# Moving the context feed-forward's buffers, and its operand preparation, in a two-layer hybrid transformer kernel on one Trainium2 core

## The chip, the cores and the metric

The kernel runs on one core of one Trainium2 chip. The metric is device time in microseconds for one execution, the median of several. The core has five engines with a queue of instructions each: TensorE (PE in the profile: matmuls, with its weight loads listed as PEld), VectorE (DVE), ScalarE (ACT), GpSimd (POOL) and SyncE (SP, which here only issues transfers). An engine runs its own instructions strictly in order; semaphores make it wait for others. Transfers between HBM and SBUF are carried by 16 DMA engines.

## What is computed

Two layers over a latent sequence of 1024 tokens (`x`) and a context of 256 tokens (`ctx`), width 1024, all in float32. Each layer: modulated RMS norm, a mixer (layer 0 recurrent, layer 1 attention), a gated residual, and a convolutional feed-forward with a gated residual. The modulation vectors come from the conditioning vectors by one matrix of 1024 x 6144 a layer. What bears on this case is the end of layer 0:

```python
def _ada(cond, w, b):
    m = (jax.nn.silu(cond) @ w + b)[:, None, :]
    return jnp.split(m, 6, axis=-1)

def _conv_ffn(h, w_up, conv_w, w_down):          # D_FF = 2816
    gate, val = jnp.split(h @ w_up, 2, axis=-1)
    gate = _dwconv(gate, conv_w)
    return (jax.nn.silu(gate) * val) @ w_down

for i in range(DEPTH):                           # DEPTH = 2
    ...
    x = x + ml[2] * mix_l
    x = x + ml[5] * _conv_ffn(_modulate(_rms(x), ml[3], ml[4]), ffn_w_up[i], ffn_conv[i], ffn_w_down[i])
    if not last:
        ctx = ctx + mc[2] * mix_c
        ctx = ctx + mc[5] * _conv_ffn(_modulate(_rms(ctx), mc[3], mc[4]), ffn_w_up[i], ffn_conv[i], ffn_w_down[i])
return _rms(x) * final_norm
```

## The kernel before

The kernel is one straight program in stages. Those around the change are, in program order:

- **Mixer output** (lines 1263 to 1325): the output projection of layer 0's mixer, first for the context chunk (`ci` 0, plain float32), then for the two latent chunks (`ci` 1 and 2, each float32 operand split in a high and a low part, three matmuls a product by `mm3`, lines 155 to 157). `m_in(0)` loads the context's mixer result into the tile `m0`, `m_in(1)` and `m_in(2)` go through the load buffers `mt`. In this stage the operand `hx` of the next one is made.
- **Context feed-forward** (lines 1328 to 1349, with `ffn_ctx`, lines 1207 to 1253): 22 steps `step(f)`, one for each 128 hidden columns. A step loads the gate's and the value's 1024 x 128 weights in two buffers of 256 KB each, multiplies them with `hx` (line 1220, tile `fg`) and applies convolution, SiLU and product on ACT and DVE (tile `ft`). Every fourth step, and the last, multiplies the finished groups by their down weights (`downs`, line 1230, tile `fd`) and adds the result to `xT[0]`. A float32 matmul shows as two records.
- Two generators are advanced between the steps. `mods` (`mod_chain`, `mod_steps`) makes the modulation vectors of layer 1: 24 pieces of 8 rows each, 192 advances; an advance loads 128 KB from GpSimd's queue (line 217, tile `mw`) and multiplies and adds it on DVE into `macc`, for both conditioning vectors in the first 8 pieces and for one in the others; a piece ends with matmuls (line 230, tile `mps`) that run when the next piece is at its second advance. `prep` (`ffn_prep`) makes the operands of the next stage from `xT[1]` and `xT[2]`: 20 advances, each some work on ACT, DVE, GpSimd and a few matmuls, through the scratch tiles `rm_sq`, `rm_rs`, `rm_dg`.
- Inside a step `fill()` advances `mods` by two, twice a step and twice more in each `downs`; after a step, `prep` is advanced by one and `mods` by four.
- **First feed-forward** (lines 1350 to 1377, `ffn_run`): layer 0's feed-forward on the 1024 latent tokens, again 22 steps `up(f)`, by seven products of split operands each. `up(f)` loads the two weight tiles (`st`, 512 KB each), splits them into `w0h`/`w0l` (gate) and `w1h`/`w1l` (value) by a cast on ACT (line 1100) and a subtraction on GpSimd, then adds and subtracts the two weight tiles in place on DVE (`st<-st`, line 94) and splits each result (`s0` to `s3`, line 1109). The products with `w0` come first, then `s0`, `s1`, ... After `up(0)` the hook `ctx_out` normalises the finished context and writes it out.

Order and memory are not written out by hand. A scheduler lays out each engine's queue by simulating the program: an instruction goes in as soon as its operands and its buffer are free, the earlier in program order first. Pools of SBUF tiles are stacks: a pool opened with `side="right"` is put below the right stack, any other on top of the left stack, in the order of the calls, and a pool's buffers are used in turn. A tile on an address that a closed pool had waits for the earlier tiles there, tile by tile (`reuse_waits="tile"`), and for nothing else.

In bytes of a partition, from the shapes: the left stack holds 14,048 bytes (constants and `xT0`), then `h0` with `m0` and `hx` (8,192 each). On it the mixer output stage puts `tmpc` (10,304), `fstc` and `fstw` (8,192 each: the two buffers of the input and of the weight loads), then `mi` (four `mt`), `wo`, `mpc`. The context stage puts `fsta` (11 weight buffers of 2,048), `mpa` (four `macc`, six `mw`, 10,240), `fga` (six `ft`, 6,144), `fta` (2,048) and `tmpa` (`prep`'s scratch, 10,304), up to 81,696. The right stack comes down to 81,888 with `xT1`, `xT2` and the operands of the first feed-forward. Below that come, when the context stage is over, the first feed-forward's own pools: `fst0` (load buffers, 10,240), `fw0` (split weights, 28,672, in the order `w0h`, `w0l`, `w1h`, `w1l`, `s0h` to `s3l` from below), `ft0` (12,320).

Of the kernel before, what the change touches and what calls it, by code (L numbers as in the profile page):

```python
# [9 lines left out]
F32 = mybir.dt.float32  # L10
# [9 lines left out]
KD = 8  # L20
# [50 lines left out]
def kernel(  # L71
# [9 lines left out]
    def dma(o, i):  # L81
        o = o.bitcast(F32) if o.dtype == F32R else o
        i = i.bitcast(F32) if i.dtype == F32R else i
        nc.sync.dma_start(out=o, in_=i)

    def dump(name, ap):
        if dbg is not None and name in dbg:
            dma(dbg[name], ap)
# [4 lines left out]
    def tt(e, o, a, b, op):  # L93
        e.tensor_tensor(out=o, in0=a, in1=b, op=op)  # L94
# [7 lines left out]
    def stt(e, o, a, s, b, op0, op1):  # L102
        e.scalar_tensor_tensor(out=o, in0=a, scalar=s, in1=b, op0=op0, op1=op1)  # L103

    def pool(stack, name, bufs, psum=False, side=None):
        kw = {"space": PSUM} if psum else {}
        return stack.enter_context(tc.tile_pool(name=name, bufs=bufs, reuse_waits="tile", side=side, **kw))
# [37 lines left out]
    def evac(i, o, a):  # L145
        if i % 2 == 0:
            S.copy(out=o, in_=a)
        else:
            V.tensor_copy(out=o, in_=a)

    def hilo(pl, shape, name):
        return [pl.tile(shape, F32R, tag=f"{name}{e}", name=f"{name}{e}") for e in "hl"]

    def mm3(ps, wh, wl, xh, xl, first, last):
        T.matmul(ps, lhsT=wh, rhs=xh, start=first, stop=False)  # L155
        T.matmul(ps, lhsT=wh, rhs=xl, start=False, stop=False)  # L156
        T.matmul(ps, lhsT=wl, rhs=xh, start=False, stop=last)  # L157

    def split(hi, lo, src, lo_eng=None):
        S.copy(out=hi, in_=src)  # L160
        tt(lo_eng or G, lo, src, hi.bitcast(F32), ALU.subtract)
# [39 lines left out]
    def rms_mod(tmp, psp, tag, xt, n, s1, sh, hi, lo, w=256):  # L201
        for p0 in range(0, n, w):
            xs = xt[:, :, p0:p0 + w]
            r, sq = normalised(tmp, psp, tag, xs)
            tt(V, sq, xs, r, ALU.mult)
            if lo is None:
                scale_shift(hi[:, :, p0:p0 + w], sq, s1, sh)
            else:
                modulate(sq, s1, sh, hi[:, :, p0:p0 + w], lo[:, :, p0:p0 + w])
# [45 lines left out]
    def mod_acc(*a):  # L255
        for _ in mod_steps(*a):
            pass

    def mcol(l, d, idx):
        return modc[l][d][:, idx * 8:idx * 8 + 8]  # L260
# [14 lines left out]
    with ExitStack() as p0:  # L275
        ini = p0.enter_context(tc.tile_pool(name="ini", bufs=1, reuse_waits="tile"))
        ld = p0.enter_context(tc.tile_pool(name="ld", bufs=2, reuse_waits="tile"))
        tmp = p0.enter_context(tc.tile_pool(name="tmp0", bufs=1, reuse_waits="tile"))
# [743 lines left out]
    def ffn_ops(pl):  # L1022
        Ah = hilo(pl, [128, KD, 2, 256], "a")
        Bh = hilo(pl, [128, 4, 2, 256], "b")
        return Ah, Bh, [hilo(pl, [128, 4, 2, 256], f"t{i}") for i in range(4)]
# [50 lines left out]
    def load(p, src):  # L1076
        st = p.st.tile([128, KD, 128], F32, tag="st", name="st")
        dma(st, src)
        return st
# [178 lines left out]
    if True:  # L1258
        fa, fc = Ffn(), Ffn()
        xp0 = pool(p0, "xp0", 1)  # L1260
        xT[0] = xp0.tile([128, KD, NCTX], F32, name="xT0")
        h0 = pool(h0s, "h0", 1)
        with ExitStack() as po:
            hC = pool(po, "hC", 1, side="right")
            tmp = pool(po, "tmpc", 1)
            fc.st = pool(po, "fstc", 2)
            fw = Ffn()
            fw.st = pool(po, "fstw", 2)
            mi = pool(po, "mi", 4)
            wo = pool(po, "wo", 5)  # L1270
            mp = pool(po, "mpc", 1)
            mhl = {}
            def x_in(g):
                src = ctx_in[0, g:g + 128] if g < NCTX else x[0, g - NCTX:g - NCTX + 128]
                ci, o = (0, g) if g < NCTX else ((g - NCTX) // 512 + 1, (g - NCTX) % 512)
                xin = load(fc, src.rearrange("p (k m) -> p k m", m=128))
                for hf in range(2):
                    ps = pd.tile([128, 4, 128], F32, tag="d", name="xtr")
                    for k in range(4):
                        T.transpose(ps[:, k], xin[:, hf * 4 + k], ident)  # L1280
                    evac(hf, xT[ci][:, hf * 4:hf * 4 + 4, o:o + 128], ps)

            xs_ = iter(range(0, NT, 128))
            def m_in(ci):
                t0, n = CHUNKS[ci]
                if ci == 0:
                    mf = mhl[0] = h0.tile([128, KD, n], F32, tag="m0h", name="m0")
                    for k in KORD:
                        dma(mf[:, k], m_scr[k, :, t0:t0 + n])
                    return  # L1290
                mh, ml_ = mhl[ci] = hilo(hC, [128, KD, n], f"m{ci}")
                for k in KORD:
                    mt = mi.tile([128, 512], F32, tag="mt", name="mt")
                    dma(mt[:, 0:n], m_scr[k, :, t0:t0 + n])
                    S.copy(out=mh[:, k], in_=mt[:, 0:n])
                    tt(V, ml_[:, k], mt[:, 0:n], mh[:, k].bitcast(F32), ALU.subtract)
            for ci in (0, 1, 2):
                m_in(ci)
            for _ in range(6):
                x_in(next(xs_))  # L1300
            for ci in (0, 1, 2):
                t0, n = CHUNKS[ci]
                d = 1 if ci == 0 else 0
                if ci not in (0, 1, 2):
                    m_in(ci)
                for dt in range(KD):
                    st = load(fw, rec_w_out[0, :, dt * 128:(dt + 1) * 128].rearrange("(k p) m -> p k m", p=128))
                    ps = pu.tile([128, 512], F32, tag="u", name="po")
                    if ci == 0:
                        for i, k in enumerate(KORD):  # L1310
                            T.matmul(ps[:, 0:n], lhsT=st[:, k], rhs=mhl[0][:, k], start=i == 0, stop=i == KD - 1)
                    else:
                        mh, ml_ = mhl[ci]
                        wh, wl = hilo(wo, [128, KD, 128], "wo")
                        split(wh, wl, st)
                        for i, k in enumerate(KORD):
                            mm3(ps[:, 0:n], wh[:, k], wl[:, k], mh[:, k], ml_[:, k], i == 0, i == KD - 1)
                    stt(V, xT[ci][:, dt], ps[:, 0:n], mcol(0, d, 2)[:, dt:dt + 1], xT[ci][:, dt], ALU.mult, ALU.add)
                    for _ in range({(0, d): 1 for d in range(2, 6)}.get((ci, dt), 0)):
                        x_in(next(xs_))  # L1320
                dump(f"xmix{ci}", xT[ci])
                mod_acc(mp, pd, "d", 0, (4, 3, 5)[ci], (0, 1), 0, 1024)
                if ci == 1:
                    hx = h0.tile([128, KD, NCTX], F32, tag="m0l", name="hx")
                    rms_mod(tmp, pd, "d", xT[0], NCTX, mcol(0, 1, 4), mcol(0, 1, 3), hx, None, w=128)
        if stop == "C":
            return
        hEs = ExitStack()
        ops = ffn_ops(pool(hEs, "hE0", 1, side="right"))
        with ExitStack() as pf:  # L1330
            fa.st = pool(pf, "fsta", 11)
            mp = pool(pf, "mpa", 1)
            mods = mod_chain([(mp, pd, "d", 1, i, (0, 1) if i < 2 else (0,), q, 256, 6, nc.gpsimd) for i in (1, 0, 2, 4, 3, 5) for q in range(4)])
            fa.g = pool(pf, "fga", 6)
            fa.t = pool(pf, "fta", 2)
            step = ffn_ctx(fa, hx, lambda: (next(mods, None), next(mods, None)))
            tmp = pool(pf, "tmpa", 1)
            prep = (None for ci in (1, 2) for _ in ffn_prep(0, ops, tmp, ci, 128))
            for f in range(NF):
                step(f)  # L1340
                next(prep, None)
                for _ in range(4):
                    next(mods, None)
            for _ in prep:
                pass
            for _ in mods:
                pass
            dump("xf0_0", xT[0])
        h0s.close()
    pf = ExitStack()  # L1350
# [30 lines left out]
    with ExitStack() as pq:  # L1381
# [5 lines left out]
        with ExitStack() as pqq:  # L1387
# [35 lines left out]
            with ExitStack() as pt_q:  # L1423
                tmp = pool(pt_q, "tmpq", 2, side="right")
# [179 lines left out]
    with ExitStack() as pe:  # L1604
# [3 lines left out]
        with ExitStack() as pr_:  # L1608
            tmp = pool(pr_, "tmpe", 1)
# [65 lines left out]
```

## Time and profile before

| | us |
|---|---|
| median of 3 runs | 3424.66 (3417.45 to 3427.35) |
| the profiled execution | 3425.41 |
| span of the profiled execution's instructions | 3423.6 |
| PE busy, share of the span | 93% |
| DVE, POOL, ACT busy | 70%, 45%, 38% |

A view of the profile is either a total (busy time of an engine, of a group of instructions, of a stretch of the span) or an order of events (the timeline, where each row is a run of equal instructions on one engine, with the idle time before it in brackets and what ended it). PE's busy time is modelled and says little about how full PE is; the count of matmuls in a stretch says more. Times in the timeline are microseconds from the span's start; the context feed-forward runs from 1122 to 1383.

### The profile page before, as it was taken

How to read it: one execution, taken by the hardware profiler on the slowest of the kernel's cores; microseconds unless marked ns; L12 is line 12 of the kernel's file. 1: busy time of each engine (PE TensorE's matmuls, PEld its weight loads, DVE VectorE, ACT ScalarE, POOL GpSimd, SP SyncE). 2: the span in 40 equal slices, each digit the busy share in tenths (PEclk: the TensorE clock that was granted, in tenths of full speed). 3: DMA queues.
4: the chain of work that ended last, by engine and by line, in shares of the span. 5: the costliest groups of instructions: out<-in, count | busy, mean ns of one | idle time of the engine just before them, and what ended most of it. 6: DMA issues, size and time to landing. Idle time of an engine off the chain costs nothing. (4 is left out here: it accounts for less than half of the span.)

```text
span 3423.6 us, 47533 instructions
## 1 busy us (share of the span) xinstructions
PE 3188.8 (93%) x16708; PEld 2667.4 (78%) x16708; DVE 2394.2 (70%) x4177; ACT 1309.6 (38%) x2982; POOL 1535.8 (45%) x1459
## 2 busy tenths in 40 slices
PE   7988988899979999899999997999999799999998
PEld 4776877777768888688887877988888678887877
DVE  5567467568767877777767777467567667777677
ACT  4434242644421222333333323557566433333333
POOL 2232231233215455565555643753434555655554
PEclk9998999999979999999999998999999899999999
DMA  5445444645586677211121121330111111111211
GB/s 185 112 123 162 135 128 126 185 146 166 178 267 198 192 242 229 72 56 44 53 59 50 56 71 45 105 90 26 50 44 35 28 53 50 56 44 53 59 50 71
DMA packets 438508, 350.14 MB, mean 102 GB/s; under 512 B 57556, under 2 KB 385470, under 8 KB 437758
## 3 DMA queue, kind: packets, MB, share of 16 engines
q1 hardware_dynamic: 429054, 321.93, 31.6%
q0 software_dynamic: 9216, 25.18, 2.3%
q8 instruction: 132, 2.16, 0.3%
q14 instruction: 106, 0.87, 0.1%
HBM read 286.25 MB, written 60.76 MB: 101 GB/s over the span
## 5 line engine op out<-in xcount | busy, mean ns | idle before, releaser
L103 DVE SCALAR_TENSOR_TENSOR xT<-fd,mod,xT 128x512 f32<-128x512 f32 (+1 forms) x432 | 291.4, 694 | 192.7 <-PE fd L157 170.5
L155 PE MATMUL pj<-hhi,whi 128*128 128x512 f32 (+1 forms) x696 | 263.8, 379 | 22.2 <-ACT raw L525 13.1
L156 PE MATMUL fd<-gl,dh 128*128 128x512 f32 (+1 forms) x688 | 266.7, 388 | 6.1 <-DVE gl L94 6.0
L157 PE MATMUL fd<-gh,dl 128*128 128x512 f32 (+1 forms) x688 | 266.1, 387 | 0.0
L155 PE MATMUL fd<-gh,dh 128*128 128x512 f32 (+1 forms) x688 | 262.0, 391 | 0.6 <-ACT gh L1155 0.3
L156 PE MATMUL pj<-hlo,whi 128*128 128x512 f32 (+1 forms) x696 | 260.9, 375 | 0.3 <-DVE hlo L94 0.3
L157 PE MATMUL pj<-hhi,wlo 128*128 128x512 f32 (+1 forms) x696 | 259.4, 373 | 0.0
L94 DVE TENSOR_TENSOR st<-st 128x512 f32<-128x512 f32 x176 | 211.7, 1204 | 51.2 <-POOL s1l L94 39.2
L103 DVE SCALAR_TENSOR_TENSOR macc<-mw,sc,macc 128x256 f32<-128x256 f32 (+1 forms) x322 | 206.9, 668 | 32.5 <-DMA mw<-in_mod_w_dram 30.9
L100 POOL TENSOR_SCALAR P<-P,rc 128x512 f32<-128x512 f32 (+1 forms) x192 | 116.7, 626 | 200.0 <-DVE rc L1539 57.6
L94 POOL TENSOR_TENSOR dl<-sd,dh 128x256 fp32r<-128x256 f32 x168 | 157.0, 950 | 108.3 <-ACT dh L160 108.3
L94 POOL TENSOR_TENSOR wlo<-wst,whi 128x512 fp32r<-128x512 f32 x58 | 77.2, 1332 | 270.3 <-ACT whi L160 269.8
L94 POOL TENSOR_TENSOR w0l<-st,w0h 128x1024 fp32r<-128x1024 f32 x44 | 105.7, 2402 | 153.4 <-ACT w0h L1100 145.5
L155 PEld LDWEIGHTS pj<-hhi,whi 128*128 128x128 f32 x696 | 137.9, 198 | 46.8 <-ACT raw L525 15.4
L1220 PE MATMUL fg<-hx,st 128*128 128x256 f32 x704 | 162.8, 380 | 3.7 <-DMA st<-in_ffn_w_up_dram 3.1
L217 POOL DMA_DIRECT2D mw<-in_mod_w_dram x192 | 105.0, 548 | 121.6 <-DVE macc L103 50.2
L156 PEld LDWEIGHTS fd<-gl,dh 128*128 128x128 f32 x688 | 129.6, 188 | 37.9 <-DVE gl L94 11.4
L94 POOL TENSOR_TENSOR p<-p,u 128x512 f32<-128x512 f32 (+1 forms) x45 | 93.3, 2073 | 143.6 <-DVE u L94 143.6
L103 DVE SCALAR_TENSOR_TENSOR ft<-fraw,conv_f,ft 128x1024 f32<-128x1024 f32 x88 | 134.7, 1530 | 30.8 <-ACT ft L91 30.1
L155 PEld LDWEIGHTS fd<-gh,dh 128*128 128x128 f32 x688 | 128.3, 188 | 33.8 <-ACT gh L1155 7.9
L156 PEld LDWEIGHTS pj<-hlo,whi 128*128 128x128 f32 x696 | 138.3, 199 | 18.7 <-DVE hlo L94 0.7
L157 PEld LDWEIGHTS pj<-hhi,wlo 128*128 128x128 f32 x696 | 137.9, 198 | 18.8 <-issue 0.2
(610 smaller groups left out, 9857.3 us busy)
## 6 DMA issues: line engine op xcount, KB each, us to landing
st<-in_ffn_w_up_dram SPq DMA_DIRECT2D x88, 512.0 KB
mw<-in_mod_w_dram POOLq DMA_DIRECT2D x192, 128.0 KB, 3.7
st<-in_ffn_w_up_dram SPq DMA_DIRECT2D x88, 256.0 KB
sd<-in_ffn_w_down_dram SPq DMA_DIRECT2D x176, 128.0 KB
sh<-sh_scr SPq DMA_DIRECT2D x80, 256.0 KB
wst<-in_rec_w_in_dram SPq DMA_DIRECT2D x56, 256.0 KB
st<-in_rec_w_out_dram SPq DMA_DIRECT2D x24, 512.0 KB
mw<-in_mod_w_dram SPq DMA_DIRECT2D x24, 512.0 KB
```

The source lines that it names most:

```text
L94: e.tensor_tensor(out=o, in0=a, in1=b, op=op)
L100: e.tensor_scalar(out=o, in0=a, scalar1=s1, scalar2=s2, op0=op0, op1=op1)
L103: e.scalar_tensor_tensor(out=o, in0=a, scalar=s, in1=b, op0=op0, op1=op1)
L155: T.matmul(ps, lhsT=wh, rhs=xh, start=first, stop=False)
L156: T.matmul(ps, lhsT=wh, rhs=xl, start=False, stop=False)
L157: T.matmul(ps, lhsT=wl, rhs=xh, start=False, stop=last)
L217: (eng or nc.sync).dma_start(out=w, in_=mod_w[l, k * 128:(k + 1) * 128, c0:c0 + width])
L1220: T.matmul(ps, lhsT=h[k // 4][:, k % 4], rhs=hx[:, k], start=k == 0, stop=k == KD - 1)
```

## The change

`m0` gets a pool of its own in the mixer output stage, `m0p`, behind `fstw`, so that `h0` holds only `hx` and everything above starts 8,192 bytes lower. In the context stage the weight buffers become 9 in place of 11, and the order of the pools is `fsta`, `fta`, `tmpa`, `mpa`, `fga`. After each step `prep` is advanced by two in place of one, so that its 20 advances end after the tenth step; `mods` is advanced by two after each of the first 11 steps and by six after each of the others, in place of four after each. The sum of all calls stays the same.

```diff
@@ -1266,6 +1266,7 @@
             fw.st = pool(po, "fstw", 2)
+            m0p = pool(po, "m0p", 1)
             mi = pool(po, "mi", 4)
@@ -1284,7 +1285,7 @@
                 if ci == 0:
-                    mf = mhl[0] = h0.tile([128, KD, n], F32, tag="m0h", name="m0")
+                    mf = mhl[0] = m0p.tile([128, KD, n], F32, tag="m0h", name="m0")
@@ -1328,18 +1329,19 @@
         with ExitStack() as pf:
-            fa.st = pool(pf, "fsta", 11)
+            fa.st = pool(pf, "fsta", 9)
+            fa.t = pool(pf, "fta", 2)
+            tmp = pool(pf, "tmpa", 1)
             mp = pool(pf, "mpa", 1)
             mods = mod_chain([...])
             fa.g = pool(pf, "fga", 6)
-            fa.t = pool(pf, "fta", 2)
             step = ffn_ctx(fa, hx, lambda: (next(mods, None), next(mods, None)))
-            tmp = pool(pf, "tmpa", 1)
             prep = (None for ci in (1, 2) for _ in ffn_prep(0, ops, tmp, ci, 128))
             for f in range(NF):
                 step(f)
-                next(prep, None)
-                for _ in range(4):
+                for _ in range(2):
+                    next(prep, None)
+                for _ in range(2 if f < 11 else 6):
                     next(mods, None)
```

By the shapes the context stage's pools now lie from 22,240 up: `fsta` to 40,672, `fta` to 42,720, `tmpa` to 53,024, `mpa` to 63,264, `fga` to 69,408. The first feed-forward's pools stay where they were: `fst0` from 71,648, `fw0` from 42,976 (`w0h` and `w0l` up to 51,168, `w1` up to 55,264, the rest above), `ft0` from 30,656.

## Rows read from the trace of the kernel before

**Rows 1.** The page's first block: busy time, share of the span, instructions.

```profile
PE 3188.8 (93%) x16708; PEld 2667.4 (78%) x16708; DVE 2394.2 (70%) x4177; ACT 1309.6 (38%) x2982; POOL 1535.8 (45%) x1459
```

**Rows 2.** Busy time (and count) by stretch; the first row names the columns.

```profile
core 0: us, PE busy (x) PEld busy (x) DVE busy (x) ACT busy (x) POOL busy (x), PEclk, DMA share, GB/s
1055.00:1094.00 39.00, 39.00 (x176) 32.36 (x175) 25.50 (x27) 10.45 (x15) 23.52 (x14) 0.91 0.52 162
...
1122.00:1252.00 130.00, 128.21 (x638) 112.51 (x638) 116.25 (x278) 30.17 (x61) 64.59 (x107) 1.00 0.73 220
1252.00:1383.00 131.00, 123.19 (x584) 106.67 (x582) 93.72 (x216) 25.21 (x52) 59.89 (x101) 0.99 0.68 208
1383.00:1411.00 28.00, 25.49 (x113) 20.38 (x114) 22.42 (x30) 15.36 (x29) 19.39 (x18) 1.00 0.33 96
1411.00:1424.00 13.00, 8.54 (x28) 6.11 (x27) 10.96 (x11) 4.93 (x8) 8.21 (x6) 0.74 0.27 77
...
1470.00:1500.00 30.00, 30.00 (x134) 24.83 (x133) 20.11 (x25) 9.87 (x17) 14.64 (x12) 1.00 0.21 62
```

**Rows 3.** PE's waits from 1090 to 1450: total us, times, longest.

```profile
PE fg L1220 <- DMA st<-in_ffn_w_up_dram: 3.1, 5, 1.0
PE fg L157 <- POOL s1l L94: 2.0, 1, 2.0
```

**Rows 4.** Timeline around the end of the context stage: start, us, instruction, [idle before].

```profile
1354.80 13.98 PE L1230 MATMUL fd<-ft,st 128*128 128x256 f32 x64
...
1362.31 0.68 DVE L94 TENSOR_TENSOR t3l<-rm_sq,t3h 128x512 fp32r<-128x512 f32 x1
1363.02 1.00 SPq L84 DMA_DIRECT2D st<-in_ffn_w_up_dram  x2
...
1373.43 1.23 PE L230 MATMUL mps<-ones,macc 128*128 128x128 f32 x4 [4.21 <-DVE macc L103]
...
1382.20 1.04 ACT L1100 CAST w0h<-st 128x1024 fp32r<-128x1024 f32 x1 [24.73 <-PE fd L1230]
...
1383.29 0.50 PE L155 MATMUL fg<-ah,w0h 128*128 128x512 f32 x1 [0.70 <-ACT w0h L1100]
1383.32 2.38 POOL L94 TENSOR_TENSOR w0l<-st,w0h 128x1024 fp32r<-128x1024 f32 x1 [12.37 <-ACT w0h L1100]
...
1385.76 0.50 PE L157 MATMUL fg<-ah,w0l 128*128 128x512 f32 x1 [1.26 <-POOL w0l L94]
```

**Rows 5.** Timeline where the second step `up(1)` meets the hook `ctx_out`.

```profile
1413.79 1.41 DVE L94 TENSOR_TENSOR st<-st 128x512 f32<-128x512 f32 x2
...
1415.85 0.80 PE L155 MATMUL fg<-t0h,s0h 128*128 128x512 f32 x1 [3.80 <-ACT s0h L1109]
...
1417.73 0.79 PE L157 MATMUL fg<-t0h,s0l 128*128 128x512 f32 x1 [0.66 <-POOL s0l L94]
```

**Rows 6.** Timeline before the context stage: a wait, the first `mw`, the first `prep`.

```profile
995.50 0.80 PE L1311 MATMUL po<-m,st 128*128 128x256 f32 x1 [3.74 <-DMA st<-in_rec_w_out_dram]
...
1094.93 3.42 POOL L217 DMA_DIRECT2D mw<-in_mod_w_dram  x6 [0.33 <-POOL wol L94]
...
1113.18 2.01 ACT L91 ACTIVATE rm_sq<-xT 128x1024 f32<-128x1024 f32 x2 [21.36 <-PE po L156]
```

**Rows 7.** Tile `rm_sq` alone by stretch: DVE, ACT, POOL busy, PEclk, DMA, GB/s.

```profile
1122.00:1252.00 130.00, 32.14 (x35) 19.53 (x36) 13.98 (x15) 1.00 0.73 220
1252.00:1383.00 131.00, 20.69 (x29) 16.50 (x32) 12.16 (x14) 0.99 0.68 208
```

**Rows 8.** Groups of instructions, DVE, 1122 to 1383: count | busy, mean ns.

```profile
L103 DVE SCALAR_TENSOR_TENSOR macc<-mw,sc,macc 128x256 f32<-128x256 f32 x196 | 99.0, 518 | 10.1 <-DMA mw<-in_mod_w_dram 8.6
```

**Rows 9.** DMA queues, 1252 to 1370: packets, MB, share (q1 SyncE, q0 GpSimd).

```profile
q1 hardware_dynamic: 24195, 15.96, 46.0%
q0 software_dynamic: 4035, 11.02, 28.9%
```

**Rows 10.** Tile `mw` alone, the stretch of most traffic: DVE, POOL, PEclk, DMA, GB/s.

```profile
1330.00:1342.00 12.00, 6.54 (x14) 7.66 (x14) 1.00 0.91 296
```

## The prediction

> **What bounds the kernel now.** First the page's busy times: PE is busy for 93% of the span and no other engine for more than 70% [rows 1], so a change pays only where PE stands still or runs slowly, and the question is where PE does so around the context stage. The stretches answer that [rows 2]: in the first half of the context stage PE idles for 130 - 128.2 = 1.8 us, in the second for 131 - 123.2 = 7.8 us; at the start of the first feed-forward it idles for 28 - 25.5 = 2.5 us, and in the 13 us from 1411 it does 28 matmuls. At the full rate of the stretch from 1470 (134 in 30 us, 0.224 us each) those are 6.3 us, so 6.7 us are lost there. Some 19 us, 0.55% of the span, is all that can be won in this place. Then the waits and the timeline, for the causes. In the context stage: 4.21 us before the last `mps`, whose `macc` is late on DVE [rows 4], and 3.1 us in five short waits for weights, the longest 1.0 [rows 3]. At the start: 0.70 for `w0h` and 1.26 for `w0l` [rows 4]. In `up(1)`: 3.80 and 0.66 us for the `s0` split, with a granted clock of 0.74 on the mean of that stretch: for a part of it, after the long wait, PE ran at 1.2 in place of 2.4 GHz [rows 2, 5]. In `up(2)`: 2.0 for `s1l` [rows 3].
>
> The start is late because of memory. The loads of the first weights go out at 1363.02, just when `prep` has read its scratch for the last time (`t3l`, 1362.31 plus 0.68), since `fst0` lies on that scratch; the cast `w0h` stands 24.73 us and runs when PE has read its last context weights, since `fw0` begins on `fsta` [rows 4]. So tiles wait for what lay on their own bytes and for nothing else. The `mw` loads and the first `prep` show the same: they run 27 and 9 us before the stage's first matmul at 1122, as soon as the weight split (`wol`) or PE frees the bytes under them [rows 6].
>
> **The change part by part**, against the profiled execution's 3425.41 us (span 3423.6 and 1.8 around it, 0.75 above the median of 3424.66).
>
> (a) First weights. `fst0` now lies on nothing of the stage, so its 1 MB can be loaded any time; `w0h` and `w0l` lie on `prep`'s scratch, free when `prep` ends. `prep` ends after step 10 of 22 in program order, so both splits (1.04 and 2.38 us) fit into ACT and POOL, which are busy for 25 and 60 of 131 us in the second half [rows 2, 4]. PE's 0.70 and 1.26 us go: -2.0. What is late next: nothing on PE before `s0`. `w1` and `s0` still lie on `macc`, and the chain to `s0` (cast, subtraction, add, cast, subtraction) can be done only behind the last `mps`; on tiles half as large as `w0` a cast is some 0.5 and a subtraction 1.2 us, an add is 0.7 [rows 4, 5], 4.1 us in all. But then 16 context products follow (half of the 64 records of 13.98 us, 7 us) and the 24 with `w0` (24 x 0.224 = 5.4 us): covered.
>
> (b) `up(1)`. Its `s0` waits for two adds that DVE does at 1413.79 [rows 5], behind `ctx_out`. With the chain of `up(0)` moved forward, its four adds of 0.7 us leave DVE's queue there, 2.8 us; `ctx_out` starts a little earlier, but PE also comes 2 us earlier. Of the 6.7 us lost I take half, -3.3; the ends are 0 and -6.7, and a further -2.0 for `up(2)`, where I see no reason and take 0.
>
> (c) The last `mps`. DVE has no `prep` left in the second half, which brings `macc` earlier; but after step 20 there are now 12 `mods` advances (six, four in step 21, two in the last `downs`) where there were 8, all in DVE's order between additions that wait for PE. I take -1.0; ends -4.2 and +4.2.
>
> (d) Two weight buffers fewer. A buffer is eight records, 8 x 13.98 / 64 = 1.75 us of PE [rows 4]; the cover falls from 19 to 16 us. If the five waits grow as the cover shrinks, 3.1 x 11/9 = 3.8: +0.7; if each grows by a whole buffer, +8.7; if they vanish, because SP has nothing else to do, -3.1. The waits' mean of 0.6 is nearer to the first: +1.0.
>
> (e) DVE in the first half. It is busy for 116.25 of 130 us; the scratch work of the second half, 20.7 us, comes on top [rows 2, 7]: 136.9, more than there is. Against that `mods` falls from 96 advances (11 x 8 and twice 4) to 74, 22 fewer at 0.518 us: -11.4 us, 125.5 of 130 [rows 8]. DVE has also 13.5 us idle from 1055 to 1094, and `mods` can use that now: `mw` and `macc` no longer lie on the load buffers of the output weights, which held them until 1094.93, but on `mt` and `m0`, which nothing reads after `ci` 0 [rows 2, 6]. So DVE just fits, but with less slack for the PSUM buffers that PE fills and DVE empties. +1.0; ends -1.0 and +7 (the 136.9 if nothing is displaced).
>
> (f) The six early `mw` loads, 0.79 MB, can now go out where PE waits 3.74 us for weights at 995 [rows 6]; at 296 GB/s [rows 10] they take 2.7 us: ends 0 and +2.7, taken +0.5. `m0p` itself costs nothing: `m0` and the moved load buffers wait for the same projection as before.
>
> The sum: -2.0 - 3.3 - 1.0 + 1.0 + 1.0 + 0.5 = -3.8, that is 3421.6 us.
>
> **The rivals.**
>
> Slower: the weights starve in the second half. By program order it gets 118 `mods` advances, 22 more, 2.9 MB. From 1252 to 1370 the queues moved 16.0 + 11.0 = 27.0 MB, 229 GB/s [rows 9]; 29.9 would be 253, where the fullest 12 us show 296 and a DMA share of 0.91 [rows 10], and PE's weights alone want 262 KB in 1.75 us, 150 GB/s. If each added load of 131 KB (0.44 us at 296) delays the weights by its own length, as it would with nothing left to cover, that is 9.7 us, and a late last `mps` costs 4.2 more: with (a) and (b), -5.3, and (d) to (f), +2.5, it gives +11.1, 3436.5. It decides from the point where the two queues want more than 296 GB/s together through a run of up products, not on the mean. Against it: the mean stays 15% below that, and early `mods` take part of the 22 away. Here a rule of the Trainium skill speaks against the change: its page "DMA: Bandwidth & Descriptors", section "Queues, rings and completion order", says that a DMA engine takes the queues that have work in turn, a packet each. SyncE's packets have 660 bytes on the mean and GpSimd's 2731 [rows 9], so by that rule, with both always full, the weights would get a fifth of the bytes, 58 GB/s of 296. The trace does not bear that out for long stretches: the weights got 59% of the bytes. The page's rule makes bursts of `mods` dearer; the sum goes without it.
>
> Faster, by more: the whole loss at the start goes, and `mods` ends in time. -2.0 - 6.7 - 4.2 + 1.0 (d) + 1.0 (e) = -10.9, 3414.5, and with `up(2)`'s 2.0 or the five waits some 3 less: about 3412. For it: DVE's second half falls from 94 to about 80 of 131 us. Against it: `macc` is held up by DVE's order, not by DVE's load; the backlog behind `ctx_out` stays, apart from four adds.
>
> The change does not do what it says: the scheduler puts the splits behind the last context work all the same, or `s0` is next to be late. Then only (c) to (f) are left, +1.5: 3427.
>
> **How the numbers follow.** 0.3% is 10.3 us, about what a measurement of this kernel can tell from no change. The forecast, a gain under that, including small losses from a first half that is too full: 0.50. The splits do not move, 3427, or (b) gives nothing: 0.06, also within. Faster: 0.27. Slower by starved weights: 0.17. So faster by over 0.3% 0.27, within 0.56, slower 0.17. The best ends that do not exclude each other, -2 - 8.7 - 4.2 - 3.1, give 3407, and the order of the queues, laid anew from 1000 on, some us beyond; the slower case stands at 3436.5. To leave out no more than two in ten I take 3406 to 3438; the forecast's own range is 3415 to 3432.
>
> **What would show each step.** (a): casts `w0h`, `w0l` before the last `fd` and no PE wait for them at the stage's end. (b): the stretch from `up(1)`'s start with under 3 us lost. (c): the wait before the last `mps` under 4 us. (d), rival one: PE's waits for `in_ffn_w_up` stay near 4 us, or reach 10. (e): DVE busy over 120 of the first 130 us, PE idle there under 4 us, `mw` loads before 1090. (f): PE's waits for `in_rec_w_out` not above those before. I am wrong if the stage from 1122 to the first `fg<-ah,w0h` grows by more than 5 us, or if it shrinks by more than 8.

## The result and the profile after

| | before | after |
|---|---|---|
| median of four runs, us | 3424.78 | 3456.30 |
| lowest and highest, us | 3417.45, 3427.35 | 3447.00, 3460.96 |
| profiled execution (span), us | 3425.41 (3423.6) | 3460.96 (3459.2) |

The ratio is 1.0093, 95% interval 1.0078 to 1.0108: 32 us slower, where the prediction said 3 us faster and its range ended at 3438. The profiled execution of the changed kernel is the longest of its four, 4.7 us above the median, so stage lengths read from it are some us too long. Three single executions (one each of the kernel before, late9old and ownring_old) took 8.6 to 17.5 ms; the ratios below leave them out, the medians do not. Lines of the changed file stand one or two lower than before (L1311 is L1312).

First the place. The timelines of the two profiled executions give the start of each stage, in us:

| | first `po` of `ci` 0 | first `fg<-hx` | first `fg<-ah,w0h` | `s0` of `up(1)` | first `qps` | last instruction |
|---|---|---|---|---|---|---|
| before | 969.86 | 1122.24 | 1383.29 | 1415.85 | 2082.6 | 3423.6 |
| after | 971.35 | 1132.42 | 1418.84 | 1451.66 | 2118.5 | 3459.2 |

The mixer-output stage takes 161.1 us in place of 152.4, the context stage 286.4 in place of 261.1, the start of the feed-forward 32.8 in place of 32.6; behind that all is shifted by 35.6 to 35.9 us. So two losses are to be explained, 9 and 25 us, and a gain that did not come.

Busy times by stretch of the changed kernel, the columns as in [rows 2]; the context stage is cut into its first 130 us and the 131 behind them, with 20 us from the end of the first part between them:

```profile
core 0: us, PE busy (x) PEld busy (x) DVE busy (x) ACT busy (x) POOL busy (x), PEclk, DMA share, GB/s
...
1055.00:1094.00 39.00, 33.97 (x158) 27.74 (x157) 38.08 (x41) 7.34 (x7) 24.90 (x20) 0.91 0.64 187
...
1132.00:1262.00 130.00, 109.61 (x481) 92.23 (x482) 107.05 (x233) 38.86 (x76) 52.74 (x78) 0.87 0.47 142
...
1240.00:1260.00 20.00, 13.31 (x43) 10.67 (x44) 15.16 (x22) 4.82 (x8) 6.87 (x10) 0.61 0.20 60
...
1262.00:1393.00 131.00, 126.95 (x616) 112.29 (x615) 87.29 (x217) 14.75 (x32) 64.96 (x116) 0.99 0.81 246
```

Two things are to be seen. PE idles for 20 us in the first half (1.8 before, [rows 2]) and runs at a granted clock of 0.87, with 481 matmuls done where 638 were; in the second half it idles for 4 us in place of 7.8. And over that first half nothing is short by its busy time: DVE has 107 of 130 us, less than the 116 before, DMA a share of 0.47. That is a mean: from 1228 to 1248 DVE is busy without a break (20.00 us). In the mixer output, from 1055 to 1094, it is DVE that has filled up, from 25.5 to 38.1 of 39 us.

PE's waits from 1100 to 1450 (total us, times, longest), as in [rows 3]:

```profile
PE fg L1220 <- DMA st<-in_ffn_w_up_dram: 17.1, 6, 4.0
PE rm_ps L173 <- DVE rm_rs L169: 5.8, 2, 3.9
PE rm_ps L180 <- DVE rm_dg L98: 2.1, 2, 1.2
```

The waits for weights went from 3.1 us to 17.1, and from 1240 to 1260 DMA has a share of 0.20. The timeline shows how (SPq is SyncE's DMA queue; the second number of its rows is the time over which it issued so many loads):

```profile
1209.42 14.87 SPq L84 DMA_DIRECT2D st<-in_ffn_w_down_dram  x8
1226.55 35.90 SPq L84 DMA_DIRECT2D st<-in_ffn_w_up_dram  x8
...
1230.45 2.65 PE L1220 MATMUL fg<-hx,st 128*128 128x256 f32 x8 [2.23 <-DMA st<-in_ffn_w_up_dram]
1235.89 3.78 PE L1220 MATMUL fg<-hx,st 128*128 128x256 f32 x8 [2.79 <-DMA st<-in_ffn_w_up_dram]
1242.78 3.78 PE L1220 MATMUL fg<-hx,st 128*128 128x256 f32 x8 [3.11 <-DMA st<-in_ffn_w_up_dram]
1250.47 0.77 PE L173 MATMUL rm_ps<-ones,rm_rs 128*128 128x128 f32 x2 [3.90 <-DVE rm_rs L169]
1251.03 5.82 PE L1230 MATMUL fd<-ft,st 128*128 128x256 f32 x16
1256.68 0.38 PE L180 MATMUL rm_ps<-rm_dg,ones 128*128 128x128 f32 x2
1256.90 1.89 PE L1220 MATMUL fg<-hx,st 128*128 128x256 f32 x8
```

Eight of the nine buffers fill with down weights from 1209 to 1224; their first product `fd` runs at 1251. Until then PE's order has three more up tiles ahead of it, and they pass one after another through the ninth buffer: load, product, load. A tile (eight records) takes 6.9 us, of which 3.78 are the product itself at half clock; at 1256.90, at full clock, eight such records take 1.89. And behind those tiles PE waits 3.90 us more, for a reduction of `prep`.

The mixer-output stage, from the timelines of four engines after:

```profile
1020.97 3.41 POOL L217 DMA_DIRECT2D mw<-in_mod_w_dram  x6
1021.61 12.43 SPq L217 DMA_DIRECT2D mw<-in_mod_w_dram  x3
1023.36 5.83 DVE L98 TENSOR_SCALAR mod<-mod 128x8 f32<-128x8 f32 x1
1024.40 4.75 POOL L94 TENSOR_TENSOR wol<-st,woh 128x1024 fp32r<-128x1024 f32 x2
...
1034.14 2.00 SPq L84 DMA_DIRECT2D st<-in_rec_w_out_dram  x2
...
1039.89 1.05 ACT L160 CAST woh<-st 128x1024 fp32r<-128x1024 f32 x1 [13.34 <-DMA st<-in_rec_w_out_dram]
...
1085.12 2.34 POOL L94 TENSOR_TENSOR wol<-st,woh 128x1024 fp32r<-128x1024 f32 x1
1085.17 2.37 DVE L98 TENSOR_SCALAR rm_dg<-ident,rm_cs 128x128 f32<-128x128 f32 x1 [0.40 <-POOL rm_cs L176]
1087.60 0.79 PE L180 MATMUL rm_ps<-rm_dg,ones 128*128 128x128 f32 x2 [5.03 <-DVE rm_dg L98]
```

and the rows of before that answer to the third and to the last but one:

```profile
1021.65 0.46 DVE L98 TENSOR_SCALAR mod<-mod 128x8 f32<-128x8 f32 x1
1074.93 0.29 DVE L98 TENSOR_SCALAR rm_dg<-ident,rm_cs 128x128 f32<-128x128 f32 x1 [0.45 <-POOL rm_cs L176]
```

The first six `mw` loads of the context stage go out at 1020.97, 74 us earlier than in [rows 6], behind GpSimd's first weight split, when `ci` 0 has read `m0`. Their additions then lie in DVE's order between those of the modulation that belongs to this stage (`macc` 128x1024). SyncE holds that modulation's `mw` loads, in order, ahead of the loads of the output weights; three of them take 12.43 us to go out, ACT then stands 13.34 us for the weights of a `woh`, and at 1087.60 PE waits 5.03 us for a `rm_dg` whose chain stands behind `macc` on DVE. Of these 5.03 us some 2.1 are the `rm_dg` itself: it took 2.37 us (0.29 before), beside a `wol` subtraction on GpSimd.

The end of the stage:

```profile
1410.61 1.03 ACT L1100 CAST w0h<-st 128x1024 fp32r<-128x1024 f32 x1
...
1411.78 2.35 POOL L94 TENSOR_TENSOR w0l<-st,w0h 128x1024 fp32r<-128x1024 f32 x1 [6.15 <-ACT w0h L1100]
...
1418.84 0.58 PE L155 MATMUL fg<-ah,w0h 128*128 128x512 f32 x1
...
1426.05 0.50 PE L155 MATMUL fg<-t0h,s0h 128*128 128x512 f32 x1 [0.76 <-ACT s0h L1109]
...
1449.88 1.40 DVE L94 TENSOR_TENSOR st<-st 128x512 f32<-128x512 f32 x2
...
1451.66 0.50 PE L155 MATMUL fg<-t0h,s0h 128*128 128x512 f32 x1 [3.52 <-ACT s0h L1109]
```

The first weights are split ahead of the last context products and PE waits for neither; but `up(1)` waits for `s0` as long as before [rows 5], because DVE still does its two additions only when `ctx_out` is done. And in `up(0)` PE now waits for `s0`, 0.76 us for `s0h` and 0.62 for `s0l`, which it did not do before the change: DVE does the additions for it at 1424.66, behind the first two reductions of `ctx_out`.

### The profile page after: what moved, and what is told of

Its sections match the earlier page's. It is cut to its first block, busy times and chain, and to the rows that moved or that the text cites. A ratio compares the mean times of both kernels' runs of the same rounds, so it can differ in the third digit from the quotient of the medians.

```text
span 3459.2 us, 47548 instructions
## 1 busy us (share of the span) xinstructions
PE 3202.7 (93%) x16708; PEld 2673.8 (77%) x16708; DVE 2407.5 (70%) x4177; ACT 1309.2 (38%) x2982; POOL 1537.6 (44%) x1459
## 4 chain that ended last, share of the span: by engine, by line
PE 64%; DVE 17%; DMA 6%; POOL 4%; ACT 4%; issue 3%; SPq 1%; DVEq 0%; ACTq 0%; POOLq 0%
PE fg L157 6%; PE fg L155 6%; PE fg L156 6%; PE fd L156 4%; PE fd L157 4%; PE fd L155 4%; PE fg L1220 4%; PE fd L1230 2%; PE apo L155 2%; PE apo L157 2%; PE pj L155 2%; PE apo L156 2%; PE pj L156 2%; PE pj L157 2%; PE apt L1555 2%
## 5 line engine op out<-in xcount | busy, mean ns | idle before, releaser
L1220 PE MATMUL fg<-hx,st 128*128 128x256 f32 x704 | 173.1, 398 | 17.1 <-DMA st<-in_ffn_w_up_dram 17.1
L1220 PEld LDWEIGHTS fg<-hx,st 128*128 128x128 f32 x704 | 137.2, 200 | 38.3 <-DMA st<-in_ffn_w_up_dram 9.4
```

What stands on the lines that cost most here:

```text
L1220: T.matmul(ps, lhsT=h[k // 4][:, k % 4], rhs=hx[:, k], start=k == 0, stop=k == KD - 1)
```

## The experiments

Three things were changed at once, and the layout moved a fourth, the start of the modulation. The runs take them apart. "Late" below means this edit, which gives the modulation its old start and leaves all else (`macc` lies on the output weights' load buffers again):

```diff
             fc.st = pool(po, "fstc", 2)
             fw = Ffn()
-            fw.st = pool(po, "fstw", 2)
             m0p = pool(po, "m0p", 1)
+            fw.st = pool(po, "fstw", 2)
```

"Old rates" means one `next(prep, None)` and four of `mods` a step; "new rates" are the change's. Eleven buffers are `fsta` 11 with `fga` ahead of `mpa` and `tmpa` last. All results in one table; the ratio is to runs of the kernel before on the same chip, the stages are from the profiled executions (mixer output: first `po` of `ci` 0 to first `fg<-hx`; context: from there to first `fg<-ah,w0h`), "waits" are PE's for `in_ffn_w_up` up to the end of the context stage, and "tiles" counts, in the order of PE's instructions, the up tiles that stand between a group's last up tile loaded ahead of its eight down tiles and its first down product (one ring of nine only).

| run | modulation, buffers, prep, mods | median us | ratio | interval | mixer | context | waits | tiles |
|---|---|---|---|---|---|---|---|---|
| (before) | late, 11, 1, 4 | 3424.8 | 1 | | 152.4 | 261.1 | 3.1 | |
| (after) | early, 9, 2, 2/6 | 3456.3 | 1.0093 | 1.0078 to 1.0108 | 161.1 | 286.4 | 17.1 | 7 |
| late9new | late, 9, 2, 2/6 | 3446.6 | 1.0070 | 1.0053 to 1.0087 | 152.5 | 287.3 | 21.1 | 8 |
| late9old | late, 9, 1, 4 | 3424.0 | 0.9996 | 0.9982 to 1.0009 | 150.8 | 259.0 | 3.4 | 1 |
| late11new | late, 11, 2, 2/6 | 3444.1 | 1.0057 | 1.0034 to 1.0079 | 151.4 | 282.6 | 7.8 | |
| late11old | late, 11, 1, 4 | 3428.1 | 1.0010 | 0.9996 to 1.0023 | 151.6 | 262.4 | 4.1 | |
| early9old | early, 9, 1, 4 | 3429.9 | 1.0014 | 1.0004 to 1.0023 | 162.8 | 259.3 | 3.5 | 1 |
| prep2mods4 | late, 9, 2, 4 | 3454.6 | 1.0092 | 1.0077 to 1.0107 | 150.7 | 297.5 | 20.8 | 10 |
| prep1mods26 | late, 9, 1, 2/6 | 3430.8 | 1.0018 | 1.0006 to 1.0029 | 152.5 | 262.2 | 7.0 | 3 |
| prep2mods08 | late, 9, 2, 0/8 | 3465.7 | 1.0119 | 1.0104 to 1.0134 | 150.0 | 303.6 | 26.2 | 10 |
| pace15_m4 | late, 9, 1.5, 4 | 3445.4 | 1.0081 | 1.0052 to 1.0110 | 152.4 | 280.9 | 15.1 | 8 |
| ownring_new | late, 5+4, 2, 2/6 | 3452.0 | 1.0088 | 1.0067 to 1.0109 | 150.6 | 288.6 | 0 | |
| ownring_early | early, 5+4, 2, 2/6 | 3463.0 | 1.0126 | 1.0110 to 1.0142 | 160.8 | 288.1 | 0 | |
| ownring_old | late, 5+4, 1, 4 | 3429.0 | 1.0014 | 1.0001 to 1.0028 | 151.7 | 265.4 | 0 | |
| scratch4_new | late, 9, 2, 2/6, four `rm_sq` | 3433.4 | 1.0031 | 1.0016 to 1.0046 | 152.9 | 269.3 | 5.2 | 2 |
| scratch4_old | late, 9, 1, 4, four `rm_sq` | 3419.2 | 0.9996 | 0.9980 to 1.0011 | 151.3 | 258.0 | 0.9 | 0 |

**One part at a time.** late9new is the changed kernel with the edit above alone.

> The changed kernel with the pools m0p and fstw exchanged in memory, so that macc of the context stage lies on the last output weights' load buffer again: the first mw loads go out behind the last weight split, as before the change, and the order inside the mixer-output stage is the old one. Nine weight buffers and the doubled prep rate stay. Theory A (the early modulation work is the whole cause): 3422, and the context stage 261 us long as before. Theory B (too few buffers) and theory C (doubled prep rate): the 10 us of the mixer-output stage come back, the context stage stays at some 286 us, 3446. Rival on record (weights starved by bandwidth in the second half): 3446 too, with the loss behind step 11.

> As the run before, and also the old rates (one advance of prep and four of mods a step): of the change only the nine buffers and the free memory under the first feed-forward's load buffers are left. Theory B (nine buffers make SyncE and TensorE wait for one another): 3440 or more, PE's waits for in_ffn_w_up above 10 us. Theory C (the rate): 3423 to 3426, these waits at 3 to 5 us. Theory A: 3423 to 3426.

> Late modulation, eleven buffers again (fga ahead of mpa, tmpa last), the doubled prep rate stays. Theory B: 3420 to 3426, waits for in_ffn_w_up under 5 us. Theory C: 3440 or more, PE waits for rm_rs and rm_dg of prep above 5 us in the first half of the context stage, or DVE late with the conv. Theory A: 3420 to 3426.

> Late modulation, eleven buffers, old rates: only the arrangement of the memory is left, in which the load buffers of the first feed-forward lie on nothing but the end of prep's scratch. All theories: 3422 to 3426. The prediction's step (a) would give up to -2.0 if w0h and w0l are split before the last fd; the changed kernel's trace says they are split 2 us before the end of the context products, which was enough to take both waits away.

late9new takes back the mixer output to the microsecond (152.5) and leaves the context stage as it was in the changed kernel (287.3). So there are two causes, and theory A holds for the first stage only. late9old, the same with the old rates, is the kernel before in time: nine buffers cost nothing at the old rates, theory B falls. late11new, with the buffers given back, keeps 16 of 25 us (1.0057 against 1.0010, 1.0070 against 0.9996): it is the rates, theory C. Whether the two buffers make up the other 9 us under the new rates is not clear of the noise (the intervals of 1.0057 and 1.0070 overlap). late11old shows that the memory arrangement by itself gives nothing that can be measured. The recorded rival, weights starved by bandwidth in the second half, falls with late9new too: its second 131 us do 615 matmuls, where the second half of the stage before did 584, at a DMA share of 0.82 (0.68 before).

```profile
1123.00:1253.00 130.00, 109.05 (x477) 91.98 (x478) 106.97 (x235) 36.71 (x71) 52.97 (x78) 0.87 0.48 144
1253.00:1384.00 131.00, 126.86 (x615) 112.23 (x614) 88.58 (x217) 16.93 (x37) 65.36 (x117) 0.99 0.82 245
```

**The rates apart, and the early modulation apart.** The edits are the two loops: `range(2)` for `prep` with `range(4)` for `mods`; one `next(prep, None)` with `range(2 if f < 11 else 6)`; `range(2)` with `range(0 if f < 11 else 8)`. early9old is the changed kernel with the old rates.

> Late modulation, nine buffers, prep at two advances a step, mods at the old four. Against 3424.0 for the old rates and 3446.6 for the new ones. Theory P (the pace of prep: its long DVE steps stand twice as dense ahead of the conv, the products of the down weights come late, and those weights hold eight of nine buffers): 3444 to 3452, more than with two mods, since DVE has 11 us more to do in that half; PE's waits for in_ffn_w_up 15 us or more. Theory M (six mods a step in the second half): 3422 to 3428.

> Late modulation, nine buffers, prep at the old one advance a step, mods at two and six. Theory P: 3420 to 3428, waits for in_ffn_w_up under 6 us. Theory M, and the rival on record (weights starved in the second half): 3438 or more, with the loss behind step 11.

> Late modulation, nine buffers, prep at two advances a step, no mods in the first eleven steps and eight in each later one: DVE is relieved of 11.4 us (22 x 0.518) where prep is dense. If what counts under theory P is DVE's load in the first half: 3430 to 3438, with the waits for in_ffn_w_up under 10 us. If it is prep's own chain (reduction, PE, GpSimd, DVE) in PE's order: 3444 or more, as with two mods. Theory M: 3446 or more, the loss in the second half.

> The changed kernel with the old rates alone: early modulation, nine buffers, one advance of prep and four of mods. If the early mw and macc cost 10 us in the mixer-output stage whatever comes behind: 3434. If they pay that back in the context stage (less macc to do there): 3424 to 3428. If they need the dense prep behind them to do harm: 3424.

Dense `prep` is the costly one: 33 us (1.0092 against 0.9996). The shift of `mods` alone costs 7.5 by the ratios, whose intervals touch, and 3 by the stage's length, on the second half (PE idles for 10 us there); in the first half PE does not idle any more (130.00 of 130 us busy from 1124 on). Under dense `prep` the same shift saves 7.5 (1.0092 to 1.0070, intervals that overlap). prep2mods08, with still less `macc` in the first half, has the longest context stage of all, and not by its second half alone: PE idles for 15 us up to 1262 and for 19 from there to 1421. Less load on DVE did not help; in prep2mods4, too, four up tiles pass one at a time from 1228 to 1253 while DVE is busy for 5.4 of the 10 us from 1235. That prep2mods08 reached 3444 or more speaks for a chain in PE's order and against load; that it came out slower than with two `mods` was not expected, and part of its loss is not `prep`'s: from 1369 on four up tiles pass one at a time again, 90 us behind the last `t3l` (1278.38). early9old: the 9 to 12 us in the mixer output (after against late9new, early9old against late9old) come whatever follows, and the context stage, with some `macc` done ahead of it, is not shorter for it (259.3 against 259.0). Its median is up by 6 only; between the first `fg<-ah,w0h` and the first `qps` its profiled execution takes 699.7 us (699.3 in the kernel before) where late9old's takes 703.6, which no run explains.

**A theory that fell: the ring.** The column "tiles" follows the losses closely, and each tile costs some 5 us in the timeline above. So the next runs gave the down weights buffers of their own in the same memory:

```diff
-            fa.st = pool(pf, "fsta", 9)
+            fa.st = pool(pf, "fsta", 5)
+            fa.sd = pool(pf, "fstd", 4)
...
-                h = [weight(w_down(0, f), hf) for f in fs]
+                h = [weight(w_down(0, f), hf, p.sd) for f in fs]
```

> As late9new (3446.6: late modulation, new rates, 9 x 2 KB a partition for context weights), with the same memory in two rings: five buffers for the up weights, four for the down weights. Theory R (the single ring: eight of its nine buffers hold down weights while PE's order still has up products ahead of them, which then pass through one buffer at 6.75 us a tile in place of 1.75): the waits for in_ffn_w_up of 3 us and more go, the granted clock stays at 1.0 in the first half, and the time is 3424 to 3432. Theory P alone (prep's steps delay PE in the first half without the ring): 3442 or more, with PE waiting for rm_rs, rm_dg or the conv.

> The changed kernel (3456.3) with its nine buffers in two rings, five for up and four for down weights; early modulation and new rates stay. Theory R: 16 to 24 us come back, 3432 to 3440, and what is left to the kernel before, 8 to 15 us, is the mixer-output stage's (lengthened by 9 to 12 us by the early modulation). If both losses share one cause: 3424 to 3428. Without theory R: 3450 or more.

> As late9old (3424.0: late modulation, old rates), with two rings of five and four. The control: with the old order the nine-buffer ring is passed with one single wait of 3 us, so theory R expects 3418 to 3426. If two rings cost something by themselves (the second four down weights can only be loaded when the first four are used), 3428 to 3436.

The waits for up weights are gone, all 21 us of them, and the time is no shorter; set against the control, the loss is the same 25 us (1.0088 against 1.0014, 1.0070 against 0.9996). PE's waits of ownring_new from 1100 to 1430:

```profile
PE rm_ps L173 <- DVE rm_rs L169: 10.2, 1, 10.2
PE mps L230 <- DVE macc L103: 9.5, 3, 4.1
PE fd L1230 <- DMA st<-in_ffn_w_down_dram: 3.9, 2, 2.2
```

PE takes its up tiles quickly now and then stands at one `rm_ps` of `prep` for 10.2 us, until 1243.30; in late9new, whose waits named the weights, the same `rm_ps` (the seventh of `prep`'s eight in the stage) runs at 1245.40; both are 122.0 us behind their first `fg<-hx` (1121.26 and 1123.40). But PE has not got equally far by then: it has done 538 matmuls of the stage in ownring_new and 442 in late9new, where the controls ownring_old and late9old have done 606 and 584. So half of that backlog goes with the ring, 68 matmuls in place of 142, and the time is spent behind it: from there to the end of the stage PE idles for 18 us where late9new idles for 4. Theory R falls as the account of the time; what makes the second part longer with two rings is not shown, beyond the waits for `macc` and down weights, which the control has as well. The control has a price of its own (1.0014; 5.2 us of waits for the second four down tiles, 10.7 for `macc`), so ownring_early says only that the loss of the mixer output is there again (160.8 us against 150.6).

**The next theory: prep's chain.** In `prep` a round (four in the stage, each with `t3l` as its last split) goes through ACT, DVE, PE, GpSimd and back on one pair of `rm_sq` buffers. ACT and DVE of late9new at the seam between two rounds:

```profile
1196.02 0.62 ACT L1054 CAST t3h<-rm_sq 128x512 fp32r<-128x512 f32 x1 [0.74 <-POOL rm_sq L94]
1197.70 1.06 ACT L91 ACTIVATE rm_sq<-xT 128x1024 f32<-128x1024 f32 x1 [1.06 <-DVE t1l L94]
1198.38 0.68 DVE L94 TENSOR_TENSOR t3l<-rm_sq,t3h 128x512 fp32r<-128x512 f32 x1
1198.98 1.94 DVE L169 TENSOR_REDUCE rm_rs<-rm_sq 128x128 f32<-128x1024 f32 x1
1199.09 1.06 ACT L91 ACTIVATE rm_sq<-xT 128x1024 f32<-128x1024 f32 x1 [0.33 <-DVE t3l L94]
1201.23 1.92 DVE L169 TENSOR_REDUCE rm_rs<-rm_sq 128x128 f32<-128x1024 f32 x1
```

Each `rm_sq` of the next round waits for the last reader of its buffer (`t1l`, `t3l`). The last splits of late9new start at 1163.76, 1198.38, 1239.33 and 1295.59: 35, 41 and 56 us apart, where five advances at two a step ask for a round every 2.5 steps, 30 us (130 us of [rows 2] for 11 steps). Before they started 53, 74 and 60 us apart, with 59 asked for. scratch4 gives `rm_sq` four buffers in `tmpa` (pools in the order `fsta`, `fta`, `fga`, `mpa`, `tmpa`):

```diff
-    ... else 2 if tmp.name.startswith("tmpq") else 2)
+    ... else 4 if tmp.name.startswith("tmpa") else 2)
```

and pace15_m4 goes back to two and asks for less (`range(2 - f % 2)`, `mods` at four).

> As late9new (3446.6: late modulation, nine buffers in one ring, new rates), but prep has four rm_sq buffers in place of two, so that the next round of prep need not wait until the last split of the round before has read its scratch. Theory S (a round of prep is one chain through ACT, DVE, PE, GpSimd on one pair of scratch buffers; two advances a step ask for a round in 2.5 steps, some 30 us, and it takes 35 us and more, and TensorE's fixed order waits for it, by its own rm_ps or by the products behind it): 3424 to 3432, the fourth t3l under 150 us behind the first fg<-hx. Theory D (DVE has too much to do there whatever the scratch): 3442 or more.

> Late modulation, nine buffers, prep at one and two advances in turn (1.5 a step), mods at the old four; two rm_sq buffers. Between late9old (3424.0 at 1 a step) and prep2mods4 (3454.6 at 2). Theory S: a round is asked for every 3.3 steps, 39 us, near what its chain takes: most of the loss goes, 3424 to 3434. Theory D, in proportion to the pace: 3437 to 3442.

> The control to scratch4_new: late modulation, nine buffers, old rates, four rm_sq buffers. At one advance a step a round has 59 us and no wait for its scratch shows: 3420 to 3428 by either theory.

scratch4_new takes back half of the loss at an unchanged pace (1.0070 to 1.0031, with 0.9996 for the old rates; context stage 287.3 to 269.3, waits for weights 21.1 to 5.2), and the last round's `t3l` starts 151 us behind the first `fg<-hx` in place of 172; the control does not move. The `rm_ps` that came 122.0 us behind the first product now comes after 89.8. So that half goes with the pair of buffers. Two things weaken it: the edit moves pools as well (late11new, with the same order of pools, two `rm_sq` and eleven weight buffers, stands at 1.0057, and its interval overlaps that of 1.0031), and the profiled execution of scratch4_new is the fastest of its ten, 6.8 us below the median. The whole was expected, and did not come; nor did every round get shorter, for the four `t3l` are now 22, 41 and 41 us apart. pace15_m4 missed both theories: at three quarters of the pace the loss is nearly whole, and its `t3l` are 52, 57 and 37 us apart where 39 are asked for. PE's order has eight up tiles ahead of the down products there, as many as in late9new, and before two of these groups PE waits for the conv on DVE:

```profile
1265.22 2.62 PE L1220 MATMUL fg<-hx,st 128*128 128x256 f32 x8 [3.80 <-DVE ft L103]
1271.32 3.78 PE L1220 MATMUL fg<-hx,st 128*128 128x256 f32 x8 [3.49 <-DMA st<-in_ffn_w_up_dram]
```

So the loss does not go by the pace against the chain's length alone: where the two advances of a step fall, in the fixed orders of PE and DVE, must count too, but no run here tests that by itself. What the other half of the loss is made of, in scratch4_new, stays open; its largest waits are 5.2 us for weights and 4.1 us for a `mod` on DVE ahead of `fd`. That six `mw` loads ahead of the weight splits set off the loss in the mixer output is read from the timeline; only that the early start costs it is shown, by three pairs of runs (8.6, 12.0 and 10.2 us of stage). No version beat the kernel before.

## Why the prediction was wrong, step by step

(a) First weights, -2.0: both waits are gone in the changed kernel, but not by the reason given. With the old rates and the same layout of the context stage (late9old, early9old) they are gone as well; late11new, with the new rates and another layout, keeps 1.6 us for `w0l`, as late11old does. So it hangs on the layout, not on `prep` ending early. And "nothing on PE before `s0`" failed: 1.4 us of new waits for the `s0` of `up(0)` take most of the gain, and from the first `fg<-ah,w0h` to `up(1)` it is 32.8 us, where it was 32.6.

(b) `up(1)`, -3.3: failed, 3.52 us of wait as before. I took four additions out of DVE's queue; but the chain of `up(0)` stayed with `ctx_out`, and the two additions that count stand behind `ctx_out`'s steps in DVE's order as before. The term is 0.

(c) The last `mps`, -1.0: the wait of 4.21 us is gone in the changed kernel; under-sized by 3 us. The reason was that DVE has no `prep` left in the second half, and with the old rates the wait is nearly gone too (1.2 us of such waits in late9old), so the hit is luck in part. In late11new, with the new rates, such waits are 8.7 us: the end of +4.2 that I gave was the right sign there.

(d) Two buffers fewer, +1.0: right with the old rates. late9old against late11old is 0.9996 against 1.0010, and the waits are 3.4 and 4.1 us. With the new rates, which the step had to price, it was too low in the waits: 21.1 us with nine buffers and 7.8 with eleven. In the stage 4.7 us of that show (287.3 against 282.6), in the time nothing that is clear of the noise (1.0070 against 1.0057).

(e) DVE in the first half, +1.0, ends -1 and +7: here the prediction fell, by some 25 us. I added up DVE's busy time, found 125.5 of 130 us and took that as fitting. DVE was busy for 107, and the stage lost 25 us. What had to be costed was the pace of `prep` itself (33 us, prep2mods4 against late9old), and in it the chain, which stands for about half of the loss as far as scratch4_new shows it: a round takes 35 us and more on its one pair of buffers, and 30 were asked for. What it holds up is not DVE's sum but what stands behind it in fixed orders: `rm_ps` on PE, the conv ahead of the down products, and so eight buffers. How the other half comes about stays open. Under "what would show" I wrote DVE over 120 and PE idle under 4; both were wrong (107 and 20): PE stood still with less work on DVE, not with more.

(e) and (f), the early modulation: seen, with its right cause (`mw` and `macc` on `mt` and `m0`), and taken as a help, for DVE's 13.5 idle us, and a harm of 0.5 at most 2.7 us, by bandwidth. It costs 9 to 12 us in the mixer output (6 to 8 by the medians). The sign that (f) named did not move, PE's waits for `in_rec_w_out` are 7.5 us (7.4 before); the loss came by other waits. I named the queue that the loads enter (GpSimd's), but not who stands behind them: the weight splits there, the stage's own `macc` on DVE, and behind that one SyncE's queue with the output weights.

The slower rival had the sign and a third of the size, +11, and the wrong mechanism: starvation by traffic in the second half. The second half ran at 246 GB/s and a DMA share of 0.81 with 4 us of PE idle; most of the waits for weights lay in the first half, where from 1240 to 1260 the share was 0.20. The range reached to that rival only and so missed by 18 us.

## What to carry to other kernels

When work is moved to a denser pace, price the pace by itself, and compare the length of its own dependent chain (all engines, on its own buffers) with the interval that the new pace gives it; busy shares don't show it. Where the orders of the engines are fixed, work that can start early does start early: ask for each queue that it enters what stands behind it. And a wait for weights while DMA is idle names a symptom; before buffers are given to it, look what the next wait behind it would be: here the waits went with a second ring, and the time did not.

## What the runs showed of the hardware

A wait cost PE twice here. Where tiles passed one at a time, with PE idle for 2.8 to 3.1 us before each, the granted clock was 0.50 from 1236.00 to 1239.50, which is 1.2 GHz (0.61 on the mean from 1240 to 1260): eight records took 3.78 us. From 1256.90 to 1263.00, when PE had no such waits, it was 1.00, 2.4 GHz, and eight records took 1.89. So each wait of about 3 us cost another 1.9 us behind it.

A DVE instruction of 8 elements a partition took 5.83 us (0.46 before): it ended at 1029.19, right behind two subtractions of GpSimd that ran back to back until 1029.15, behind six `mw` loads in GpSimd's queue. The `rm_dg` of the mixer output, 2.37 us in place of 0.29, started 0.05 us behind a subtraction of GpSimd and ended 0.08 us behind its end. The Trainium skill, page "SBUF — State Buffer", section "Who interferes with whom", says that DVE and GpSimd share a pair of ports as an exclusive lock, which a DVE instruction needs when it runs in a two-port mode (`tensor_scalar` can enter one) or has two inputs in SBUF, and that the one that comes second is blocked entirely. The row of `rm_dg` agrees with that. The row of 5.83 us agrees by its end only: its record starts at 1023.36, 1.04 us ahead of the first subtraction, while GpSimd was still issuing the loads. No run here separates the lock from other causes.
